# Layer B's memory queries and gates as four more paired products kept in DRAM, and the memory attention moved ahead of the sample attention

## The chip, the cores and the metric

The kernel runs on one core of a Trainium2 chip. The metric is the time of one execution on the device in microseconds. The time of the kernel before is 1783.64 us, the median of three runs (1783.11 to 1785.19).

## What is computed

One inference step of a trunk of two layers, A and then B, for a prompt of 512 tokens and a sample group of 8 x 8 = 64 tokens; the model width is 2048. Both groups share all weights, so that most products run over 576 columns. Layer A is a convolution module and is not touched. Of layer B this matters:

```python
def _b_layer(x, attend, mem_kv, w_in, w_out, ln_g, ln_b):
    h = jnp.einsum('btd,de->bte', x, w_in)
    q, gate, qm, gm = jnp.split(h, [MIX_WIDTH, MIX_WIDTH + B_OUT, MIX_WIDTH + B_OUT + MEM_WIDTH], axis=-1)
    q = q.reshape(b, t, N_GROUPS, B_HEADS_PER_GROUP, HEAD_DIM)
    o = attend([q[:, :, g] for g in range(N_GROUPS)])
    o = o.astype(x.dtype).reshape(b, t, B_OUT) * jax.nn.silu(gate)
    m = _mem_attn(qm, mem_kv) * jax.nn.silu(gm)
    y = jnp.einsum('bte,ed->btd', jnp.concatenate([o, m], axis=-1), w_out)
    return _layernorm(ALPHA * x + y, ln_g, ln_b)
```

`attend` is a dilated sliding-window attention with three groups of four heads of 128, merged by their softmax denominators. The sample group reads its keys and values from caches (`state_kv_g0` to `g2`). `_mem_attn` is a softmax attention of four heads over 256 memory entries (`qm` are its queries, `gm` its gate): for the prompt from `mem_prompt`, for the sample from `cache_mem_kv`. Inputs and outputs are float32.

## The kernel before

**Products.** Activations stand with the features on the partitions: 16 tiles of 128 features x 576 tokens. A weight slab is [128, 2048] for 128 output features. Each float32 factor is split into a high part in fp32r (copied on ScalarE, `wh`) and the rest (subtracted on VectorE, `wl`), and a product is three matmuls: high x high, high x low, low x high. A `Unit` is one slab, that is 4 steps (quarters of the slab); a step is 4 weight tiles x 3 products x 2 column halves of 288 = 24 matmuls. A `Pair` forms two slabs at once by a scheme of the Strassen kind: the two slabs, the two halves of the features and the two halves of the tokens are 2 x 2 blocks, and 7 block products stand for 8. It has 14 sets (7 products, two parts each) of 12 matmuls of 288 columns. For them VectorE forms eight sums of weight quarters (`sum`), in places given by `SUMS`, and the sums of the activations stand ready in `combos`. The evictions are in `after`: ScalarE copies an accumulator to a snapshot tile (`st`, in one of the two weight buffers with the tag `raw`), and VectorE adds a second accumulator in the function `evs`.

**The order.** `steps` is one list, and `run_steps` emits it: the matmuls of a step, the hooks at that place, the splits of the next steps, the eviction of the step before, and then `stage_lanes`, in which each of five lanes (queues of Python generators) does its next piece up to a `yield`. A turn of the lanes behind a step is called a stage here. Each engine runs its instructions in that order.

**Layer B.** First come the queries and keys of the attention, 24 slabs: 4 as units, then 20 as 10 pairs (`n_pairs` to `n_rest`). They are evicted to SBUF, written to the DRAM tile `kept_qk` on POOL's queue, and read back by `prompt_attn` on SP's queue. Then, from `n_rest` to `n_b`, come 12 units for the values, 8 for the memory's queries and gates (`B_QM`, `B_GM`: two queries, two gates, twice) and 4 for the attention's gate, 96 steps in all. Behind them stand the output units.

In that stage the lanes do the attention. Lane 0: `prompt_attn(h)`, from the moment the values of head h are there; it takes ten stages a head. Lane 1: `samples()`, for the two pairs of heads first the keys of three groups (`sample_keys`, 12 chunks), then one chunk more and 13 chunks of values (`sample_rest`), and at the end the memory attention of the sample (`queries_mem` with `mem_sample`, 4 chunks a pair). Lane 2: transposes of the values, and the gating. Lanes 3 and 4: the prompt's memory attention (`fetch_mem`, `mem_prompt`), started by the eviction of the gate (`start_mem`), and the split of its output (`mem_out`).

**The chunks.** The sample's caches are read in chunks of [128, 2048] float32, 1 MB. `chunk_load` issues their loads on POOL's queue, in the order of `chunk_list`, into two buffers:

```python
    def chunk_load():
        while cstate["load"] < min(cstate["use"] + 2, cstate["limit"]):
            ...
            t_ = kvp[0].tile([128, 2048], F32, tag="kv", bufs=2, name=f"kv{i}")
            nc.gpsimd.dma_start(t_, src)
```

A load waits on POOL until the matmuls that read the buffer's last chunk have ended. `sample_keys` and `sample_rest` take one chunk and then yield, so that a step's 24 matmuls (and what lane 0 has) stand between two chunks. The memory's keys and values for the prompt were formed in layer A's time and lie in the DRAM tile `spill`. SP's queue carries the weights, the saved queries and keys, the bias tables (`tp_`, `tl_`) and `spill`, in the order of the program.

Of the kernel before, what the change touches and what calls it, by code (L numbers as in the profile page):

```python
# [81 lines left out]
def trunk(ctx, tc, xt, memt, wm, wa, wao, wb, wbo, cst, scv, kc, rest, mc, relb, oneh,  # L82
# [420 lines left out]
    chunk_list += [mc[0, p_, c] for p_ in range(2) for c in range(4)]  # L503
    for p_ in range(2):
        chunk_list += [kc[p_, c] for c in list(range(1, 13)) + [0] + list(range(13, 26))]
    chunk_list += [mc[1, p_, c] for p_ in range(2) for c in range(4)]
# [613 lines left out]
    def fetch_mem(pr):  # L1120
# [3 lines left out]
        for a in range(2):  # L1124
            h = 2 * pr + a
            kmem1[h] = t_[:, a, :]
            nc.sync.dma_start(kmem1[h], spill[h])
            vs.append(u([128, NMEM], name="mkv"))
            nc.sync.dma_start(vs[a], spill[4 + h])
        yield  # L1130
# [8 lines left out]
        for a in range(2 * pr):  # L1139
            for h in (2 * a, 2 * a + 1):  # L1140
                lanes[4].append(mem_out(h))
# [274 lines left out]
    def sample_keys(pr):  # L1416
# [10 lines left out]
        for i in (1, 2, 3):  # L1427
            g = 1 if i == 1 else 2
            lg = at()
            for b in range(4):  # L1430
# [4 lines left out]
                if b < 3:  # L1435
                    yield
# [4 lines left out]
    def sample_rest(pr):  # L1441
# [40 lines left out]
        for i in range(13):  # L1482
# [9 lines left out]
            yield 0.25  # L1492
# [53 lines left out]
    def ev_qmb(h):  # L1546
        def f(ps):
            t_ = qmb[h] = u([128, T], name="qmb")
            nc.scalar.activation(two(t_), cols(ps), AF.Copy, scale=SCALE)
        return f  # L1550

    def start_mem(h):
        def f(ps):
            ev_gate(gmb, h)(ps)
            if h % 2:
                mem_ok[h // 2] = True
                lanes[3].append(fetch_mem(h // 2))
        return f
# [13 lines left out]
    for i in range(N_PLAIN, len(qks), 2):  # L1572
        two_ = qks[i:i + 2]
        add_pair(Pair([wb[row_qk(*it)] for it in two_], moving, [ev_qk(*it) for it in two_],
                      1.0 if two_[0][0] else SCALE))
    n_rest = len(steps)

    def samples():
        for _ in range(2):
            yield 0.0  # L1580
        for pr in range(2):
            yield from sample_keys(pr)
            yield from sample_rest(pr)
        for pr in range(2):
            yield from queries_mem(pr)
# [14 lines left out]
    for pr in range(2):  # L1600
        for h in (2 * pr, 2 * pr + 1):
            add_unit(unit_b(B_QM + h, ev_qmb(h)))
        for h in (2 * pr, 2 * pr + 1):
            add_unit(unit_b(B_GM + h, start_mem(h)))
# [234 lines left out]
    for k in range(4, KT):  # L1839
        hooks.setdefault((k - 4) // 4 * 2 + 1, []).append(lambda k=k: x_ready(k, None))  # L1840
    for k in range(8):
# [67 lines left out]
    lanes[1].append(samples())  # L1909
    run_steps(n_b)  # L1910
# [132 lines left out]
```

## Time and profile before

| | |
|---|---|
| median of 3 runs | 1783.64 us (1783.11 to 1785.19) |
| the profiled execution, its own time | 1783.62 us |
| its span, first to last instruction | 1781.8 us |
| granted TensorE clock, mean | 0.997 |
| TensorE busy | 1764.1 us, 99% of the span |
| VectorE, ScalarE, POOL busy | 1128.1, 726.5, 150.1 us (63%, 41%, 8%) |
| DMA | 368.08 MB, mean 207 GB/s |

The profile is of one execution; its own time and its span differ by 1.8 us that lie around the instructions. PE is TensorE, PEld its weight loads, DVE VectorE, ACT ScalarE, POOL GpSimd, SP SyncE; a q behind the name is the queue's own instructions. L1433 is line 1433 of the kernel. Matmuls are pipelined and their ends are modelled, so the distance from one to the next in the chain of waits says more than the duration of one. A releaser in brackets is what ended the wait ahead of an instruction. The DMA share is the mean busy share of the core's 16 DMA engines.

### The profile page before, as it was taken

The numbers are of one execution on the slowest core, as the hardware profiler recorded it, in microseconds if no ns is written. First come the engines' busy times: TensorE is split into PE (matmuls) and PEld (weight loads), VectorE is DVE, ScalarE is ACT, GpSimd is POOL, SyncE is SP. The second block draws the span as 40 slices with busy tenths as digits, with TensorE's granted clock in tenths as the row PEclk, the third lists the DMA queues.
The fourth block names the chain that finished last, engine by engine and source line by source line (L and its number), as shares of the span: only waits on it lengthen the run. The fifth ranks groups of instructions, "written<-read, shape, count | busy, mean of one in ns | idle before, by whom it ended". The sixth has DMA issues, their size and how long they took to land.

```text
span 1781.8 us, 34785 instructions
## 1 busy us (share of the span) xinstructions
PE 1764.1 (99%) x14134; PEld 1690.0 (95%) x14134; DVE 1128.1 (63%) x1977; ACT 726.5 (41%) x1581; POOL 150.1 (8%) x271
## 2 busy tenths in 40 slices
PE   8999999999999999999999999999999999999998
PEld 8999999999999999999999999997888789999997
DVE  6977998288999784546689777761322332324666
ACT  6444444355454452223476444442322232334334
POOL 0222221000000000000010000011111110001000
PEclk9999999999999999999999999999999999999999
DMA  8575678665556456466574555469787777435312
GB/s 303 184 260 180 215 230 281 202 213 207 183 202 208 155 184 224 173 209 216 197 231 153 201 201 201 143 216 322 253 320 261 263 294 256 151 131 178 108 52 102
DMA packets 98896, 368.08 MB, mean 207 GB/s; under 512 B 17888, under 2 KB 27136, under 8 KB 87345
## 3 DMA queue, kind: packets, MB, share of 16 engines
q1 hardware_dynamic: 70752, 256.95, 43.0%
q0 software_dynamic: 24528, 105.76, 16.7%
q10 hardware_dynamic: 3456, 3.15, 0.5%
q8 instruction: 111, 1.82, 0.4%
q14 instruction: 49, 0.39, 0.1%
HBM read 335.02 MB, written 125.43 MB: 258 GB/s over the span
## 4 chain that ended last, share of the span: by engine, by line
PE 96%; DMA 2%; DVE 1%; issue 0%; ACT 0%; ACTq 0%; SPq 0%; POOL 0%; DVEq 0%; POOLq 0%
PE pp L423 73%; PE pp L234 8%; PE pp L237 4%; DMA kv<-kc 2%; PE at L1488 1%; PE at L1433 1%; PE at L618 1%; PE at L596 1%; PE at L1370 1%; PE at L1368 1%; PE at L663 0%; PE at L643 0%; PE at L611 0%; PE at L1391 0%; PE at L1381 0%
## 5 line engine op out<-in xcount | busy, mean ns | idle before, releaser
L357 ACT CAST wh<-raw 128x512 fp32r<-128x512 f32 x410 | 247.3, 617 | 359.4 <-DMA raw<-wa 141.6
L368 DVE TENSOR_TENSOR wl<-raw,wh 128x512 fp32r<-128x512 f32 x410 | 278.3, 686 | 154.9 <-ACT wh L357 76.1
L423 PE MATMUL pp<-xh,wh 128*128 128x288 f32 (+2 forms) x1408 | 307.3, 300 | 6.3 <-ACT xh L524 6.3
L423 PE MATMUL pp<-xh,wl 128*128 128x288 f32 (+2 forms) x1408 | 303.3, 297 | 0.0
L423 PE MATMUL pp<-xl,wh 128*128 128x288 f32 (+2 forms) x1408 | 303.2, 297 | 0.0
L822 DVE SCALAR_TENSOR_TENSOR conv<-ep,consts,conv 128x512 f32<-128x512 f32 x360 | 269.6, 749 | 6.9
L423 PEld LDWEIGHTS pp<-xh,wh 128*128 128x128 f32 x1408 | 234.0, 190 | 9.4 <-ACT xh L524 6.3
L423 PEld LDWEIGHTS pp<-xh,wl 128*128 128x128 f32 x1408 | 234.2, 190 | 0.0
L423 PEld LDWEIGHTS pp<-xl,wh 128*128 128x128 f32 x1408 | 233.9, 190 | 0.3 <-DVE xl L525 0.3
L423 PE MATMUL pp<-cath,wh 128*128 128x288 f32 (+2 forms) x640 | 140.5, 297 | 0.0
L423 PE MATMUL pp<-cath,wl 128*128 128x288 f32 (+2 forms) x640 | 139.7, 296 | 0.0
L423 PE MATMUL pp<-catl,wh 128*128 128x288 f32 (+2 forms) x640 | 139.5, 296 | 0.0
L423 PE MATMUL pp<-yab,wh 128*128 128x288 f32 x512 | 134.3, 305 | 0.0
L357 ACT CAST wh<-rawq 128x512 fp32r<-128x512 f32 x140 | 86.5, 620 | 84.3 <-PE pp L234 57.4
L368 DVE TENSOR_TENSOR wl<-rawq,wh 128x512 fp32r<-128x512 f32 x140 | 95.7, 686 | 26.0 <-PE pp L237 22.3
L423 PE MATMUL pp<-yb,wh 128*128 128x288 f32 x384 | 107.4, 294 | 0.0
L423 PEld LDWEIGHTS pp<-cath,wh 128*128 128x128 f32 x640 | 104.1, 189 | 0.8 <-issue 0.3
L423 PEld LDWEIGHTS pp<-cath,wl 128*128 128x128 f32 x640 | 104.0, 189 | 0.0
L423 PEld LDWEIGHTS pp<-catl,wh 128*128 128x128 f32 x640 | 104.0, 189 | 0.0
L423 PEld LDWEIGHTS pp<-yab,wh 128*128 128x128 f32 x512 | 90.7, 188 | 13.9 <-issue 10.3
L795 ACT ACTIVATE prod<-es,consts 128x64 f32<-128x64 f32 x360 | 103.0, 343 | 1.3 <-ACT mkv L563 1.3
L423 PE MATMUL pp<-yh,wh 128*128 128x288 f32 x448 | 99.8, 304 | 0.2 <-ACT yh L1245 0.2
(326 smaller groups left out, 3238.8 us busy)
## 6 DMA issues: line engine op xcount, KB each, us to landing
o_kc<-kc SPq DMA_DIRECT2D x104, 512.0 KB, 5.9
kv<-kc POOLq DMA_DIRECT2D x52, 1024.0 KB, 6.7
raw<-wa SPq DMA_DIRECT2D x86, 512.0 KB, 4.7
o_rest<-rest SPq DMA_DIRECT2D x64, 512.0 KB, 6.4
raw<-wb SPq DMA_DIRECT2D x55, 512.0 KB, 5.4
rawq<-wb SPq DMA_DIRECT2D x80, 256.0 KB, 5.3
kv<-mc POOLq DMA_DIRECT2D x16, 1024.0 KB, 5.2
raw<-wao SPq DMA_DIRECT2D x32, 512.0 KB, 4.9
```

Source lines behind the costliest of these rows:

```text
L234: nc.tensor.matmul(o, hi[:, kk * 128:(kk + 1) * 128], self.move(x, g * 4 + kk, part), start=(fresh and kk == 0 and part == 0), stop=False, ...
L237: nc.tensor.matmul(o, lo[:, kk * 128:(kk + 1) * 128], self.move(x, g * 4 + kk, 0), start=False, stop=(g == 1 and kk == 3), skip_group_chec ...
L357: nc.scalar.copy(hi, r)
L368: nc.vector.tensor_tensor(lo, r, cast(hi), op=OP.subtract)
L423: nc.tensor.matmul(un.ps[:, c, :n], w[wi], xs[k][:, c0:c0 + n], start=(q == kk == a == 0), stop=(last and kk == 3 and a == 2 and not un.tail))
L596: nc.tensor.matmul(lg[:, a * 256:(a + 1) * 256], q[:, t0:t0 + 128], kt, start=True, stop=True)
L618: nc.tensor.matmul(o[:, 0:256], vt[:, kk, :], PT[:, kk * 256:(kk + 1) * 256], start=(kk == 0), stop=(kk == 1))
L795: nc.scalar.activation(dst, es[:, :, k:k + 8], AF.Copy, scale=w)
L822: nc.vector.scalar_tensor_tensor(cv[:, 0:TP], ep[:, k:k + TP], w, cv[:, 0:TP], op0=OP.mult, op1=OP.add)
L1368: nc.tensor.matmul(o, lhs, kk, start=True, stop=True, tile_position=(0, 32 * a))
L1370: nc.tensor.matmul(lg[:, 128 + 128 * g:256 + 128 * g], q_[g, h][:, r * 128:(r + 1) * 128], k_[g, h][:, r * 128:(r + 1) * 128], start=True, ...
L1433: nc.tensor.matmul(lg[32 * rg:32 * rg + 32, :], qe[g][:, rg * 128 + b * 32:rg * 128 + b * 32 + 32], ck[:, rg, :], start=(b == 0), stop=(b ...
```

## The change

Four pairs are appended to the ten: the memory's queries of heads 0 and 1, of heads 2 and 3, then the gates of the same. Their eviction `ev_m` adds the two parts on VectorE, applies SiLU in place for a gate, and writes each head's [128, 576] tile to the new DRAM tile `kept_m` on POOL's queue. The eight units that formed them go, with `ev_qmb` and `start_mem`, so that the stage from `n_rest` to `n_b` has 64 steps. `fetch_mem` now also loads the queries and gates of its two heads on SP's queue; the first call is put on lane 3 right behind the last pair, and the first call puts the second on the lane. In `samples` the memory attention (`queries_mem`, 8 chunks, still one to a stage) comes first, and in `chunk_list` its chunks do too. `sample_keys` yields behind every second chunk, and so does `sample_rest`. The splits of the memory attention's output (`mem_out`) are started by a hook 16 steps ahead of `n_b`. The two chunk buffers stay as they are.

```diff
@@ -501,9 +501,9 @@
         return t_
 
     chunk_list += [mc[0, p_, c] for p_ in range(2) for c in range(4)]
+    chunk_list += [mc[1, p_, c] for p_ in range(2) for c in range(4)]
     for p_ in range(2):
         chunk_list += [kc[p_, c] for c in list(range(1, 13)) + [0] + list(range(13, 26))]
-    chunk_list += [mc[1, p_, c] for p_ in range(2) for c in range(4)]
 
 
     copies = [(o_rest[i], rest[i]) for i in range(32)] + [(o_kc[p_, c], kc[p_, c]) for p_ in range(2) for c in range(26)]
@@ -1127,6 +1127,10 @@
             nc.sync.dma_start(kmem1[h], spill[h])
             vs.append(u([128, NMEM], name="mkv"))
             nc.sync.dma_start(vs[a], spill[4 + h])
+            for kind, d in enumerate((qmb, gmb)):
+                d[h] = u([128, T], name="qgm")
+                nc.sync.dma_start(d[h], kept_m[kind, h])
+        mem_ok[pr] = True
         yield
         v = u([128, 2, 2, HD], name="mv")
         for a in range(2):
@@ -1136,9 +1140,8 @@
         for a in range(2):
             h = 2 * pr + a
             lanes[3 + a].append(mem_prompt(qmb[h], kmem1[h], vmem1[h], h, sink_mem))
-        for a in range(2 * pr):
-            for h in (2 * a, 2 * a + 1):
-                lanes[4].append(mem_out(h))
+        if pr == 0:
+            lanes[3].append(fetch_mem(1))
 
     def queries_mem(pr):
 
@@ -1432,7 +1435,7 @@
                 for rg in range(4):
                     nc.tensor.matmul(lg[32 * rg:32 * rg + 32, :], qe[g][:, rg * 128 + b * 32:rg * 128 + b * 32 + 32],
                                      ck[:, rg, :], start=(b == 0), stop=(b == 3), tile_position=(0, 32 * rg))
-                if b < 3:
+                if b == 1:
                     yield
             nc.vector.tensor_tensor_reduce(L[i], lg, L[i], scale=1.0, scalar=LOWEST, op0=OP.add, op1=OP.max,
                                            accum_out=mx[:, i:i + 1])
@@ -1489,7 +1492,9 @@
                                      pe[i % 2][:, rg * 128 + b * 32:rg * 128 + b * 32 + 32], cv[:, rg * 4 + b, :],
                                      start=(i == 0 and b == 0), stop=False, tile_position=(0, 32 * rg),
                                      skip_group_check=True)
-            yield 0.25
+            if i % 2:
+                yield 0.25
+        yield 0.25
         while not vdone[pr]:
             yield 0.0
 
@@ -1543,18 +1548,22 @@
 
     qmb, gmb, mob, gtb = [None] * 4, [None] * 4, [None] * 4, [None] * 4
 
-    def ev_qmb(h):
-        def f(ps):
-            t_ = qmb[h] = u([128, T], name="qmb")
-            nc.scalar.activation(two(t_), cols(ps), AF.Copy, scale=SCALE)
-        return f
-
-    def start_mem(h):
-        def f(ps):
-            ev_gate(gmb, h)(ps)
-            if h % 2:
-                mem_ok[h // 2] = True
-                lanes[3].append(fetch_mem(h // 2))
+    kept_m = tc.dram_tile([2, 4, 128, T], F32, name="kept_m")
+
+    def ev_m(kind, h):
+
+        got = {}
+
+        def f(c, src, add):
+            if not got:
+                got["t"] = u([128, T], name="m")
+            d = got["t"][:, c * 288:(c + 1) * 288]
+            nc.vector.scalar_tensor_tensor(d, src, 1.0 if kind else SCALE, add, op0=OP.mult, op1=OP.add)
+            if kind:
+                nc.scalar.activation(d, d, AF.Silu)
+            got[c] = True
+            if 0 in got and 1 in got:
+                nc.gpsimd.dma_start(kept_m[kind, h], got["t"])
         return f
 
     def unit_b(row, ev):
@@ -1573,16 +1582,20 @@
         two_ = qks[i:i + 2]
         add_pair(Pair([wb[row_qk(*it)] for it in two_], moving, [ev_qk(*it) for it in two_],
                       1.0 if two_[0][0] else SCALE))
+    for kind in range(2):
+        for h in (0, 2):
+            add_pair(Pair([wb[(B_GM if kind else B_QM) + h + a] for a in range(2)], moving,
+                          [ev_m(kind, h + a) for a in range(2)], 1.0 if kind else SCALE))
     n_rest = len(steps)
 
     def samples():
-        for _ in range(2):
+        for _ in range(3):
             yield 0.0
+        for pr in range(2):
+            yield from queries_mem(pr)
         for pr in range(2):
             yield from sample_keys(pr)
             yield from sample_rest(pr)
-        for pr in range(2):
-            yield from queries_mem(pr)
 
     first = True
     for h in range(4):
@@ -1597,11 +1610,6 @@
             un.spare = u if first else None
             first = False
             add_unit(un)
-    for pr in range(2):
-        for h in (2 * pr, 2 * pr + 1):
-            add_unit(unit_b(B_QM + h, ev_qmb(h)))
-        for h in (2 * pr, 2 * pr + 1):
-            add_unit(unit_b(B_GM + h, start_mem(h)))
     for h in range(4):
         add_unit(unit_b(B_GT + h, chain(ev_gate(gtb, h), (2, gate_o(h)))))
     n_b = len(steps)
@@ -1838,6 +1846,8 @@
         hooks.setdefault(n_mk - 10 + j, []).append(lambda j=j: sp_mem(j))
     for k in range(4, KT):
         hooks.setdefault((k - 4) // 4 * 2 + 1, []).append(lambda k=k: x_ready(k, None))
+    for h in range(4):
+        hooks.setdefault(n_b - 16, []).append(lambda h=h: lanes[4].append(mem_out(h)))
     for k in range(8):
         hooks.setdefault(n_rest - 5, []).append(lambda k=k: restore(k, 0))
         hooks.setdefault(n_rest - 1 + k // 4, []).append(lambda k=k: restore(k, 1))
@@ -1907,6 +1917,7 @@
     chunk_load()
     run_steps(n_rest)
     lanes[1].append(samples())
+    lanes[3].append(fetch_mem(0))
     run_steps(n_b)
     drain(1)
     scopes["kv"].close()
```

## Rows read from the trace of the kernel before

**Rows 1.** The page: engines over the span, and the chain that ended last.

```profile
PE 1764.1 (99%) x14134; PEld 1690.0 (95%) x14134; DVE 1128.1 (63%) x1977; ACT 726.5 (41%) x1581; POOL 150.1 (8%) x271
...
PE 96%; DMA 2%; DVE 1%; issue 0%; ACT 0%; ACTq 0%; SPq 0%; POOL 0%; DVEq 0%; POOLq 0%
```

**Rows 2.** Stretches: length, then PE, PEld, DVE, ACT, POOL busy, PEclk, DMA share, GB/s.

```profile
1038.00:1194.00 156.00, 156.00 (x1180) 156.00 (x1179) 116.10 (x207) 68.47 (x125) 13.90 (x26) 1.00 0.51 174
1206.00:1262.00 56.00, 53.40 (x399) 40.72 (x398) 11.04 (x26) 13.18 (x25) 8.09 (x15) 1.00 0.90 326
1300.00:1320.00 20.00, 19.40 (x244) 17.25 (x236) 3.63 (x9) 4.53 (x8) 2.70 (x5) 1.00 0.99 372
1366.00:1431.00 65.00, 65.00 (x522) 50.83 (x524) 17.01 (x45) 15.97 (x37) 8.12 (x15) 1.00 0.81 290
```

**Rows 3.** TensorE's groups, 1190 to 1650 us: busy, mean ns, idle before, releaser.

```profile
L1488 PE MATMUL at<-kv,pe 128*32 128x128 f32 x832 | 28.1, 276 | 0.6 <-DMA kv<-kc 0.6
L1433 PE MATMUL at<-kv,qe 128*32 128x512 f32 x192 | 25.6, 604 | 2.6 <-DMA kv<-kc 2.6
```

**Rows 4.** The chain of waits in the pairs: start us, us, what.

```profile
1150.80 1.07 PE pp L234 x8
...
1173.06 1.07 PE pp L234 x8
```

**Rows 5.** The same chain: the first value steps, and eight plain steps.

```profile
1193.74 12.74 PE pp L423 x96
...
1557.89 25.46 PE pp L423 x192
```

**Rows 6.** DMA issues, 1038 to 1262 us: KB each, us to landing.

```profile
kept_qk<-qk POOLq DMA_DIRECT2D x14, 256.0 KB, 2.8
...
kv<-kc POOLq DMA_DIRECT2D x12, 1024.0 KB, 7.3
...
L<-tl__92 SPq DMA_DIRECT2D x3, 256.0 KB, 5.6
```

**Rows 7.** The chain of waits where chunks are read, 1366 to 1503 us.

```profile
1366.93 1.00 PE at L1433 x8
1367.93 3.37 PE pp L423 x24
...
1425.71 0.99 PE at L1433 x8
...
1438.80 1.01 PE at L1488 x32
...
1502.96 1.01 PE at L1488 x32
```

**Rows 8.** The timeline: one chunk's read, and the load into its buffer.

```profile
1206.41 1.06 PE L1433 MATMUL at<-kv,qe 128*32 128x512 f32 x8
...
1207.81 0.55 POOL L492 DMA_DIRECT2D kv<-kc  x1 [9.30 <-PE at L1433]
```

**Rows 9.** Chunk loads, L492, from 1195 to 1510 and 1560 to 1600 us.

```profile
DMA to landing us min/median/max: 5.0/6.8/9.2
...
DMA to landing us min/median/max: 5.1/5.2/5.2
```

**Rows 10.** DMA queues (packets, MB, share) and chunk issues, 1366 to 1510 us.

```profile
q0 software_dynamic: 4071, 28.16, 54.4%
q1 hardware_dynamic: 4872, 12.05, 23.8%
...
kv<-kc POOLq DMA_DIRECT2D x24, 1024.0 KB, 6.5
...
kv<-mc POOLq DMA_DIRECT2D x2, 1024.0 KB, 8.7
```

**Rows 11.** The timeline of SP's queue behind the last pair.

```profile
1196.68 0.33 SPq L337 DMA_DIRECT2D raw<-wb  x1
...
1202.51 1.85 SPq L1421 DMA_DIRECT2D L<-tl__92  x4
```

## Prediction

> **What bounds the kernel now.** The page first: TensorE is busy for 99% of the span, and the chain of work that ended last is TensorE for 96% and DMA for 2% [rows 1]. So a matmul left out counts in full, as long as nothing else makes TensorE wait. Then the stretches one by one [rows 2]: from 1038 to 1194 us (layer B's pairs) TensorE never idles, VectorE has 116.10 us of 156, ScalarE 68.47, and the DMA share is 0.51. In the stage behind it, where the caches are read, VectorE and ScalarE are nearly free but the DMA queues are not: share 0.90 and 326 GB/s in the first run of key chunks, 0.99 and 372 GB/s in the densest 20 us, 0.81 later. Even so TensorE waits little there: 2.6 us before key chunks, 0.6 us before value chunks [rows 3]. That is one chunk of 1 MB to a stage, and two buffers.
>
> **The products.** One of a pair's 14 sets (12 matmuls) follows another after 1.59 us; 14 of them go from 1150.80 to 1173.06, 22.26 us [rows 4]. Eight plain steps, the work of two plain units, take 25.46 us [rows 5]. Four pairs in place of eight units: 4 x (22.26 - 25.46) = **-12.8 us**, if the pairs stay dense. VectorE's 116.10 of 156 us are 16.6 us of a pair's 22.26 [rows 2]; the new pairs' splits and weight sums are the same, their evictions no larger than the keys' now. The gates add two short SiLU passes a head, and at worst a table load, on ScalarE, which is busy for 44% there. The eight writes to DRAM go out on POOL's queue like those of the saved queries and keys, which land in 2.8 us [rows 6] and keep nobody waiting. I cost all this at nothing: TensorE's own matmuls hide it. Without that cover a pair would lose what VectorE needs beyond 22.26 us, and it has 5.6 us to spare.
>
> **What the missing steps take with them.** They are also time in which cache chunks arrive. The stage has 96 steps now and 64 afterwards. By the order of the program (each lane moves on once behind each step) the attention's keys and values are now read in 52 stages of one chunk; afterwards in 24 stages of two, in four runs, and four of one.
>
> TensorE's need: key chunks start at 1366.93 and, eleven stages on, at 1425.71, 5.34 us each with prompt attention and value transposes; value chunks go from 1438.80 to 1502.96 in twelve, 5.35 us [rows 7]. A second chunk adds 1.00 us [rows 7], so a stage of two wants **6.4 us**; bare of prompt attention 3.37 + 1.00 + 1.00 = 5.4 us.
>
> The buffer's need: the two chunks of a stage are read back to back, and the load into the second's buffer can't go out before that read has ended. A read that starts at 1206.41 takes 1.06 us, and its successor's load is issued at 1207.81, 0.34 us behind its end [rows 8]. From issue to landing a load takes 5.0 us at the least, 6.8 in the median and 9.2 at the most in this stage, and 5.1 to 5.2 where the queues are quiet [rows 9]. So the second buffer comes round in 0.34 + L + 1.06 us:
> - L = 5.1: 6.5 us, about TensorE's 6.4. Only stages bare of attention lose, 1.1 us each; three to eight of them, say 6 us in all.
> - L = 6.8: 8.2 us, 1.8 us lost in a stage.
> - L = 7.3, the median of the crowded first run [rows 6]: 8.7 us, 2.3 us lost.
>
> The first stage of each run finds both chunks loaded, which leaves 20 stages: 6, 36 or 46 us. Today the same round may take two stages, 10.7 us, which is why it is nearly hidden.
>
> A check by bytes: from 1366 to 1510 us the two queues moved 28.16 + 12.05 MB, of which 26 chunks (24 of keys and values, two of the memory [rows 10]) are 27.3; so 12.9 MB of weights, saved queries and keys, bias and outputs went beside them in 27 stages, 0.48 MB each. A stage of two needs 2.1 + 0.48 = 2.58 MB: at the best rate seen, 372 GB/s, 6.9 us, a loss of 0.5 x 20 = 11 us; in 8.2 us it is 315 GB/s, between the 290 and 326 GB/s of the two runs of key chunks [rows 2]. So L = 6.8 is what the queues deliver. Now most loads fly alone for a part of their way, then two are always under way at once, which argues against less; the wait itself spreads them, which argues against much more. **+36 us**, with 6 and 46 as bounds.
>
> By a page of the Trainium skill (DMA: Bandwidth & Descriptors, section "Anatomy of one DMA — SWDGE (gpsimd) path") a load costs a fixed 2.0 us and its bytes at 436 GB/s, an estimate of 4.4 us for a chunk; the shortest landing here is 5.0 us [rows 9]. By that figure the buffer would come round in 5.8 us, and the sum would be that of the first rival.
>
> **Smaller terms.** The waits of today go with their stages: -(2.6 + 0.6) = **-3.2 us** [rows 3]. A step behind a chunk takes 3.37 us, another 3.18 (25.46 / 8) [rows 7, 5]; 24 fewer such places give 0 to 24 x 0.19 = 4.6, I take the middle, **-2.3 us**. With two value chunks in a stage, the second's weights are transposed and copied while the first is multiplied; that copy is short, VectorE is free, and the second chunk is late anyway: nothing.
>
> The opening: the loads of the memory's keys, values, queries and gates for heads 0 and 1 are issued in the very first stage, and TensorE transposes those values one stage later. SP is not ahead there: its weight loads wait for buffers that the pairs' snapshots hold, and the second of them goes out at 1196.68; behind that one come eight new loads. The four that stand at 1202.51 now take 0.46 us each to issue [rows 11] and land after 5.6 us [rows 6]. So the sixth of the eight (head 1's values) goes out at 1196.7 + 0.3 + 5 x 0.46 = 1199.3 and lands at 1204.9; TensorE is there after two steps, 1193.74 + 6.4 = 1200.1 [rows 5]. **+4.8 us**; nothing, if SP has run ahead; 9.5, if the first read has to wait until the last gates are written. The next weights stand behind those eight loads, 3.7 us later than now, inside the same wait. For heads 2 and 3 SP has run far ahead by then: nothing. The chunk list's new order and the earlier hook for the memory's split are the same loads and operations on engines that wait: nothing.
>
> **Sum.** The profiled execution took 1783.62 us, the median of the runs is 1783.64, so nothing is corrected. 1783.6 - 12.8 - 3.2 - 2.3 + 36 + 4.8 = 1806.1: **1806 us**, 1.3% slower.
>
> **Rivals.**
> 1. *The loads stay hidden and the saving remains.* One mechanism, the time from issue to landing: at 5.1 us the buffer comes round as fast as TensorE wants it. 1783.6 - 18.3 + 6 + 0 to 4.8 = 1771 to 1776, **1774 us**, faster. For it: 5.1 us is what a load takes in quiet queues, and in the second half the median was 6.5, not 7.3 [rows 10, 6]. Against it: its partner is always under way too, and the best 20 us would already ask for 6.9 us a stage. It decides from L of about 5.7 us down, where the loss, (5.7 + 1.4 - 6.4) x 20 = 14 us, and the opening together equal the gain.
> 2. *Bandwidth alone counts.* The queues are kept full and a stage takes 6.9 us: 1783.6 - 18.3 + 11 + 4.8 = **1781 us**, no change that can be told. For it: a share of 0.99 was held for 20 us [rows 2]. Against it: with two buffers the second load is not under way while its predecessor is being read.
> 3. *Crowded throughout.* L goes to 7.3 and the opening costs 9.5: 1783.6 - 18.3 + 46 + 9.5 = **1821 us**. For it: in the first run of keys that was the median, and now twice the chunks come in a stage. Against it: the memory attention stands first, and takes the crowded opening stages with one chunk each.
> 4. *The change doesn't do what it says*: VectorE or the writes to DRAM hold the pairs up. The dense stretch speaks against it, and it would only add to the slower side; no chance of its own.
>
> **Chances.** Forecast 0.55, rival 1 0.16, rival 2 0.09, rival 3 0.20. A measurement tells 0.2% (3.6 us) from no change. Faster: rival 1 and a third of rival 2, 0.19. Same: most of the rest of rival 2, 0.05. Slower: 0.76. The range leaves out half of rival 1 below and a part of rival 3 above, about 2 in 10: 1773 to 1824 us. The forecast's own is 1794 to 1817.
>
> **What the profile would show.** Pairs: four more at 22.3 us each with no idle TensorE, so that the value units start 89 us later, near 1283 us. Opening: some us of idle TensorE before the transposes of the memory's values. Cache reading: TensorE idle for 1 to 3 us in most two-chunk stages, at the second chunk, ended by the DMA into the chunk tile, 30 to 45 us in all; a median landing of about 6.8 us; a DMA share above 0.85 in the runs. The prediction is wrong if landings stay near 5 us with two in flight, if TensorE's idle time there is under 18 us, or if the pairs' stretch shows idle TensorE.

## The result, and the profile after

The changed kernel takes 1833.24 us, median of four runs (1827.37 to 1838.5), beside 1784.2 us before: 1.026 times as long, 95% interval 1.0229 to 1.0291. The forecast was 1806 us, range 1773 to 1824: the direction is right, the loss more than twice as large as foretold, and the time outside the range. The profiled execution took 1830.15 us, 46.5 us more than that of before.

In what follows, before and after name the two kernels. TensorE by stretches (length, busy, granted clock, DMA share, GB/s): first, of before, the 500 us from the end of its pairs on; then, of after, the pairs (with the busy times of the four other engines), ten microseconds of the opening, the 410 us behind the pairs, and the same 500 us as of before:

```profile
1190.00:1690.00 500.00, 496.25 (x4595) 1.00 0.66 234
```

```profile
1038.00:1283.00 245.00, 245.00 (x1851) 245.00 (x1850) 180.99 (x318) 110.16 (x201) 19.23 (x36) 1.00 0.47 158
...
1290.00:1300.00 10.00, 5.49 (x28) 0.66 0.54 202
...
1280.00:1690.00 410.00, 362.98 (x3474) 0.95 0.71 256
1190.00:1690.00 500.00, 452.98 (x4153) 0.96 0.65 233
```

The pairs, now fourteen, run without a gap until 1283 us, 89 us later than the 1194 us of [rows 2], as foretold. Behind them TensorE is idle for 500 - 452.98 = 47.0 us, where it was idle for 3.75. And the granted clock, 1.00 there before, is 0.95 on the mean of 410 us: since its levels are 1 and 0.5 of 2.4 GHz, 410 x 0.05 / 0.5 = about 41 us at 1.2 GHz (the single stretches add up to 44).

What ended the idle time, TensorE's groups of after from 1280 to 1700 us (busy, mean ns of one, idle before and releasers):

```profile
L1491 PE MATMUL at<-kv,pe 128*32 128x128 f32 x832 | 31.1, 295 | 17.8 <-DMA kv<-kc 14.8 <-DVE wl L368 1.6 <-DVE pe L1482 1.4
L1436 PE MATMUL at<-kv,qe 128*32 128x512 f32 x192 | 28.3, 679 | 20.7 <-DMA kv<-kc 20.7
L618 PE MATMUL at<-mpt,mv 128*128 128x256 f32 x32 | 8.6, 392 | 1.8 <-DVE ob L626 1.4 <-DVE p L1388 0.5
L548 PE MATMUL at<-consts,mkv 128*128 128x128 f32 x8 | 2.0, 367 | 5.8 <-DMA mkv<-spill 5.8
```

These are the groups of [rows 3]: the wait for chunks went from 0.6 + 2.6 to 14.8 + 20.7 = 35.5 us, the opening's transposes wait 5.8, and some 5.5 us are waits that VectorE ends. The reads of the keys also became slower by themselves: 604 ns a matmul in [rows 3], 679 here. The timeline of after shows why, here TensorE alone around two stages (start, duration, what, idle before and its releaser):

```profile
1407.21 1.07 PE L1436 MATMUL at<-kv,qe 128*32 128x512 f32 x8 [1.05 <-DMA kv<-kc]
1410.34 1.34 PE L1436 MATMUL at<-kv,qe 128*32 128x512 f32 x8 [2.06 <-DMA kv<-kc]
...
1413.00 0.68 PE L423 MATMUL pp<-yl,wh 128*128 128x288 f32 x2
1413.48 0.68 PE L423 MATMUL pp<-yh,wl 128*128 128x288 f32 x2
...
1414.97 0.42 PE L423 MATMUL pp<-yh,wh 128*128 128x288 f32 x2
1415.23 0.42 PE L423 MATMUL pp<-yl,wh 128*128 128x288 f32 x2
...
1421.16 1.91 PE L1436 MATMUL at<-kv,qe 128*32 128x512 f32 x8 [2.33 <-DMA kv<-kc]
```

Ahead of 1411 us TensorE waited 1.05 and 2.06 us for the two chunks of one stage. Then a pair of plain matmuls follows its predecessor after 0.48 us; from 1414.4 us on it is 0.26 us again. The chunk read at 1421.16, behind another wait, takes 1.91 us for its 8 matmuls, not 1.07. The granted clock says the same (of the plain matmuls alone the busy time, that of their weight loads, then clock, share, GB/s):

```profile
1400.00:1405.00 5.00, 3.44 (x24) 3.20 (x24) 1.00 0.80 269
1405.00:1411.00 6.00, 0.00 (x0) 0.00 (x0) 1.00 1.00 397
1411.00:1414.40 3.40, 2.03 (x8) 2.10 (x9) 0.50 1.08 419
1414.40:1421.00 6.60, 2.31 (x18) 2.07 (x16) 1.00 1.03 389
```

There are ten such stretches between 1280 and 1690 us, one behind the opening's wait and nine behind waits for chunks. At 0.48 for 0.26 us, some 45% of a stretch is lost, 44 x 0.45 = about 20 us; by the starts of all matmuls in them it is 20 as well. Not each wait is followed by one: behind waits for chunks of 2.07 us (ahead of 1511 us) and 2.36 us (ahead of 1518 us) the clock stayed at 1.00.

So the 46.5 us are: pairs -12.8, the idle time of before -3.7, idle time of after +47.0, matmuls at 1.2 GHz about +20, and about -4 that is left over; the missing places of a step behind a chunk would lie in it.

The loop that sets the pace here, in after's chain of waits (start, us, what):

```profile
1410.34 1.36 PE at L1436 x8
1411.70 0.28 issue
1411.98 9.13 DMA kv<-kc
...
1421.16 1.94 PE at L1436 x8
1423.09 0.28 issue
1423.38 5.09 DMA kv<-kc
...
1429.91 7.75 DMA kv<-kc
```

It is read, issue, load and read again of one and the same buffer, and nothing of TensorE's other work stands in it. A round takes 11.4 us here (1411.98 to 1423.38) and 6.5 to 1429.91. In the long round the bytes have their part: the DMA share was 1.00 to 1.08 all the while (table above), and the load took 9.13 us; the next one took 5.09. The landings from 1395 to 1660 us:

```profile
DMA to landing us min/median/max: 5.0/6.5/9.4
```

### The profile page after: what moved, and what is told of

Read it like the earlier page. It is cut to its first block, busy times and chain, and to the rows that moved or that the text cites. A ratio compares the mean times of both kernels' runs of the same rounds, so it can differ in the third digit from the quotient of the medians.

```text
span 1828.4 us, 34789 instructions
## 1 busy us (share of the span) xinstructions
PE 1768.0 (97%) x14038; PEld 1691.2 (92%) x14038; DVE 1172.0 (64%) x2053; ACT 740.7 (41%) x1614; POOL 154.4 (8%) x279
## 4 chain that ended last, share of the span: by engine, by line
PE 86%; DMA 8%; issue 4%; DVE 1%; ACT 1%; POOL 0%; SPq 0%; ACTq 0%; POOLq 0%; DVEq 0%
PE pp L423 60%; PE pp L234 11%; DMA kv<-kc 6%; PE pp L237 6%; PE at L1491 1%; DMA raw<-wb 1%; PE at L1436 1%; PE at L618 1%; PE at L596 1%; PE at L643 0%; DVE wl L368 0%; PE at L663 0%; PE pp L1040 0%; PE at L964 0%; DMA mkv<-spill 0%
## 5 line engine op out<-in xcount | busy, mean ns | idle before, releaser
L357 ACT CAST wh<-raw 128x512 fp32r<-128x512 f32 x378 | 227.8, 617 | 309.4 <-DMA raw<-wa 139.2
L368 DVE TENSOR_TENSOR wl<-raw,wh 128x512 fp32r<-128x512 f32 x378 | 256.3, 685 | 127.1 <-ACT wh L357 67.7
L357 ACT CAST wh<-rawq 128x512 fp32r<-128x512 f32 x196 | 120.6, 619 | 112.3 <-PE pp L234 74.2
L368 DVE TENSOR_TENSOR wl<-rawq,wh 128x512 fp32r<-128x512 f32 x196 | 134.2, 687 | 38.1 <-PE pp L237 31.8
L423 PE MATMUL pp<-cath,wl 128*128 128x288 f32 (+2 forms) x640 | 139.7, 296 | 0.0
L234 PE MATMUL pp<-comb,wh 128*128 128x288 f32 x896 | 136.9, 294 | 0.0
L234 PEld LDWEIGHTS pp<-comb,wh 128*128 128x128 f32 x896 | 125.0, 188 | 0.0
L423 PE MATMUL pp<-yab,wh 128*128 128x288 f32 x384 | 100.5, 312 | 0.0
L423 PEld LDWEIGHTS pp<-yab,wh 128*128 128x128 f32 x384 | 69.2, 194 | 9.5 <-issue 8.5
```

Of the source, the lines that this page charges most:

```text
L234: nc.tensor.matmul(o, hi[:, kk * 128:(kk + 1) * 128], self.move(x, g * 4 + kk, part), start=(fresh and kk == 0 and part == 0), stop=False, ...
L357: nc.scalar.copy(hi, r)
L368: nc.vector.tensor_tensor(lo, r, cast(hi), op=OP.subtract)
L423: nc.tensor.matmul(un.ps[:, c, :n], w[wi], xs[k][:, c0:c0 + n], start=(q == kk == a == 0), stop=(last and kk == 3 and a == 2 and not un.tail))
```

## The experiments

The theory: each two-chunk stage waits for its buffers' round, and behind the waits the clock falls to 1.2 GHz, which costs as a second term. The rivals are named in the expectations: A, what else the change does makes the loss (the missing steps, the order); B, the queues can't deliver the bytes, whatever the buffers; C, the clock costs nothing of its own; D (from the two pairs on), any shortening of this stage is given back. Beside each run stand times of before on the same chip (medians of 1782.7 to 1787.4 us); the ratios are to those.

### The two-chunk yields alone, on the kernel before

```diff
-                if b < 3:
+                if b == 1:
                     yield
...
-            yield 0.25
+            if i % 2:
+                yield 0.25
+        yield 0.25
```

> The kernel before with one part of the change alone: the sample's keys and values are read two chunks to a stage. No pairs, the 96 steps stay, the memory attention stays last. Theory (two buffers that come round once in a stage, and a TensorE clock that falls behind the waits): the same 20 stages wait, 30 to 50 us of idle TensorE at the second chunk, granted clock below 1.00 in the stretches behind them, 1784 + 35 to 65 = 1820 to 1850 us. Rival A (the loss comes from the missing 32 steps, in which the caches' bytes arrive): all 96 steps are there, so little is lost, 1784 to 1795 us.

1836.91 us (1834.36 to 1838.93), ratio 1.0292 (1.027 to 1.0314). With all 96 steps and no new pair the loss is there in full. Its groups, and its stretches (all engines, then clock, share, GB/s):

```profile
L1488 PE MATMUL at<-kv,pe 128*32 128x128 f32 x832 | 31.5, 298 | 19.4 <-DMA kv<-kc 12.5 <-DVE new L1327 2.4 <-DVE pe L1479 2.2
L1433 PE MATMUL at<-kv,qe 128*32 128x512 f32 x192 | 28.0, 669 | 20.8 <-DMA kv<-kc 20.7
...
1190.00:1500.00 310.00, 269.82 (x2664) 226.95 (x2663) 74.77 (x208) 69.99 (x159) 37.45 (x70) 0.93 0.75 274
1500.00:1660.00 160.00, 160.00 (x1336) 151.43 (x1334) 48.81 (x114) 53.20 (x111) 6.16 (x12) 1.00 0.38 129
```

40 us of idle time and some 41 us at 1.2 GHz (ten stretches), all before 1500 us; then, to 1660 us, TensorE is never idle again, since the chunks are used up early. The loss doesn't need rival A: pairing the chunks makes the loss, with every step in place. That the missing steps would make it too, without the pairing, is what the run with one chunk to a stage shows (below).

### Useless matmuls in the wait

Ahead of the second chunk of 20 stages stand 14 matmuls that nobody reads; everything else is as in after.

```diff
+    def fill():
+        d_ = at()
+        for _ in range(14):
+            nc.tensor.matmul(d_[:, 0:288], onesr, yh[15][:, 0:288], start=True, stop=True)
...
+                if b % 2 and (i, b) != (1, 1):
+                    fill()
...
+            if i % 2 and i > 1:
+                fill()
```

> The changed kernel with work added: ahead of the second chunk of a stage (not in the first stage of a run) 14 matmuls of 288 columns whose result nobody reads, 1.8 us. Theory (the clock falls behind idle stretches and costs about 20 us of slower matmuls): the added matmuls stand mostly in time that was a wait, the granted clock stays at 1.00 in more of the stage, and the time falls although TensorE has 36 us more to do: 1815 to 1830 us, with low-clock time of under 20 us where it was 44. Rival C (the matmuls are slower because the transfers crowd them, not because of the clock): low-clock time as before, and the time rises by what of the 36 us doesn't fit into waits, 1835 to 1850 us.

1831.23 us (1827.83 to 1833.47), ratio 1.0255 (1.0229 to 1.028): as long as after, with 280 matmuls more, and 1 us above the band that the theory expected. Its groups, and its stage:

```profile
L1422 PE MATMUL at<-yh,ones 128*128 128x288 f32 x280 | 43.4, 307 | 4.1 <-DVE pe L1489 4.1
L1500 PE MATMUL at<-kv,pe 128*32 128x128 f32 x832 | 28.1, 275 | 4.5 <-DMA kv<-kc 4.4
L1443 PE MATMUL at<-kv,qe 128*32 128x512 f32 x192 | 25.8, 616 | 5.3 <-DMA kv<-kc 5.2
...
1280.00:1690.00 410.00, 387.00 (x3738) 0.99 0.71 257
```

The idle time is 23 us where it was 47, the clock 0.99, and the chunks are read at 616 and 275 ns, nearly as in [rows 3]. At 0.13 us from start to start (plain matmuls at full clock, above) the 280 are at least 37 us of work; 24 fit into idle time, and the other 13 are paid by matmuls that are back at full speed. Rival C falls: had the clock cost nothing, the kernel would be 13 us longer.

### Half chunks, split by column group

Four buffers of 0.5 MB, each freed when its half is read; for that the read goes group by group.

```diff
-            t_ = kvp[0].tile([128, 2048], F32, tag="kv", bufs=2, name=f"kv{i}")
+                t_ = kvp[0].tile([128, 1024], F32, tag="kv", bufs=4, name=f"kv{i}_{hf}")
...
-            for b in range(4):
-                for rg in range(4):
+            for rg in range(4):
+                for b in range(4):
```

> The changed kernel with each 1 MB chunk loaded as two tiles of 0.5 MB into four buffers of half the size (the same bytes, the same SBUF), and read half by half, so that a buffer is free again after half the read. Theory (the buffer's round trip is the limit): a half needs about 3.8 us from issue to landing when alone, its buffer comes round in 0.34 + 3.8 to 5 + 0.53 = 4.7 to 5.9 us, below the 6.4 us of a stage: idle TensorE at the caches falls from about 40 to under 15 us, the clock stays at 1.00 in most stretches, 1780 to 1800 us. Rival B (the queues' bandwidth is the limit): the bytes are the same and twice as many loads have to be started, so the waits stay, 1825 to 1840 us.

1862.51 us (1857.92 to 1871.3), ratio 1.0442 (1.0407 to 1.0477): a miss, some 60 us above the theory's band and above that of rival B too.

```profile
L1493 PE MATMUL at<-kv,pe 128*32 128x128 f32 x832 | 66.5, 276 | 1.4 <-DMA kv<-kc 1.1
L1438 PE MATMUL at<-kv,qe 128*32 128x512 f32 x192 | 41.1, 646 | 15.7 <-DMA kv<-kc 15.7
```

The chunk waits halved, 35.5 to 16.8 us, but the 832 value matmuls are busy for 66.5 us and not 31.1: one takes 276 ns as in [rows 3], so what they lost is running side by side. The cut changed the order of the reads along with the buffers, and tells nothing of the buffers alone.

### Half chunks, split by columns

Four buffers of 0.5 MB again, but each half holds a part of all four groups, so that the order of the groups stays; the loads have pieces of 1 KB.

```diff
+                t_ = kvp[0].tile([128, 4, 256], F32, tag="kv", bufs=4, name=f"kv{i}_{hf}")
+                nc.gpsimd.dma_start(t_, src.rearrange("p (g n) -> p g n", g=4)[:, :, hf * 256:(hf + 1) * 256])
```

> The changed kernel with each chunk in two tiles of 0.5 MB and four buffers of half the size, as in the run with half chunks, but cut so that each half holds a part of all four column groups: the four matmuls that ran side by side in the array still do, and a read takes 1.0 us again. Price: each partition's row comes in four pieces of 1 KB in place of one of 4 KB. Theory (the round trip of a buffer makes the waits): a half's buffer comes round in 0.34 + 4 to 5.5 + 0.5 = 4.8 to 6.3 us, under the 6.4 us of a stage; idle TensorE at the chunks falls from 35 to 5 to 18 us, low-clock time from 44 to under 25 us, 1790 to 1812 us. Rival B (bandwidth of the queues): 2.58 MB still have to come in a stage, in smaller pieces, so the waits are 35 us or more and the time 1830 us or more.

1840.76 us (1838.88 to 1857.62), ratio 1.0332 (1.0281 to 1.0383), and chunk waits of 38.8 us:

```profile
L1496 PE MATMUL at<-kv,pe 128*32 128x128 f32 x832 | 34.1, 299 | 19.2 <-DMA kv<-kc 17.2 <-DVE pe L1487 2.0
L1439 PE MATMUL at<-kv,qe 128*32 128x256 f32 x384 | 29.1, 407 | 21.6 <-DMA kv<-kc 21.6
```

The time and the waits are those of rival B. The theory counted on halves that land in 4 to 5.5 us; from 1400 to 1640 us they land after 6.4 us in the median, hardly sooner than the whole chunks of after (6.7). The pieces have a part in that: the queue's share was 61.8% for 50.68 MB, where after has 59.1% for 52.31, 8% more for a byte. So a finer grain of the same 2 MB doesn't help; how much of that is the bytes and how much the 1 KB pieces, this run leaves open.

### The opening two stages later

```diff
-        yield
+        for _ in range(1 if pr else 3):
+            yield
```

> The changed kernel with the first transposes of the memory's values two stages later (the loads are issued where they were). Theory (the opening waits 6.5 us for loads that are issued one stage before they are read, and the clock falls behind that wait): both go, 6.5 us and some 3 us of slow matmuls, 1833 - 10 = 1823 us; no idle TensorE before the transposes. Rival (the loads are late for another reason, as the wait for the last gates to be written): the wait is still there, 1833 us.

1833.05 us (1829.76 to 1846.09), ratio 1.0285 (1.0243 to 1.0327): no gain, and the 1823 us of the theory not met, though the wait is gone from its place.

```profile
1290.00:1300.00 10.00, 9.19 (x76) 1.00 0.79 276
...
L643 PE MATMUL at<-kv,qe 128*32 128x256 f32 x64 | 5.0, 386 | 3.5 <-DVE qe L1152 3.5
L1437 PE MATMUL at<-kv,qe 128*32 128x512 f32 x192 | 29.9, 719 | 20.2 <-DMA kv<-kc 20.2
```

The stretch that had 5.49 us of TensorE has 9.19, at full clock. But 3.5 us of waiting for the copy of the memory's queries come in place, and the chunk waits grew to 20.2 + 20.3 = 40.5: in this run the stage takes back what is won ahead of it.

### One chunk to a stage

After with the old yields, so that some 17 value chunks are left when the 64 steps are over, and are read with no product beside them.

> The changed kernel with the yields of the kernel before: one chunk to a stage. The lane then needs about 83 stages and 64 are there; what is left over, about 17 chunks of values, is read at the end of the stage with no steps in between. Theory: in the steps no waits but the opening's 6 us; at the end each chunk costs about the 2.5 to 4 us that its transfer takes, 45 to 65 us, nearly all of it idle, and the clock falls there: 1771 + 6 + 45 to 65 + 10 = 1832 to 1852 us. Rival B (the bytes set the time): whatever the order, the same loss as in the changed kernel, 1825 to 1838 us.

1832.45 us (1820.3 to 1841.04), ratio 1.0253 (1.0209 to 1.0297). Its stretch without steps (62 us), and the one with steps:

```profile
1627.00:1689.00 62.00, 35.29 (x463) 26.05 (x464) 6.53 (x19) 1.38 (x2) 7.55 (x14) 0.50 0.68 249
1400.00:1600.00 200.00, 198.20 (x1900) 167.26 (x1899) 61.74 (x163) 62.15 (x132) 22.70 (x42) 1.00 0.77 279
```

With one chunk to a stage two buffers do, 1.8 us idle in 200; the price stands at the end in one piece. So the 60 chunks cost about the same whether the 32 missing stages are missing under them or behind them. Both expectations had room for this time, so it doesn't decide between them.

### Two pairs in place of four

Heads 0 and 1 by pairs, heads 2 and 3 by the old units: 80 steps, one chunk to a stage, the memory attention behind each pair's sample attention.

```diff
-        for h in (0, 2):
+        for h in (0,):
             add_pair(Pair([wb[(B_GM if kind else B_QM) + h + a] for a in range(2)], moving,
...
+    for h in (2, 3):
+        add_unit(unit_b(B_QM + h, ev_qmb(h)))
+    for h in (2, 3):
+        add_unit(unit_b(B_GM + h, start_mem(h)))
```

> Half of the change, built so that no run of chunks needs two in a stage: only heads 0 and 1 get their memory queries and gates from pairs and DRAM, heads 2 and 3 stay units, so that 80 steps remain; the keys and values are read one chunk to a stage again, but for the first stage of each run, whose two chunks have landed before; the memory attention of each pair of heads comes behind its sample attention; the first transposes come three stages later than in the changed kernel. Theory: two pairs save 6.4 us, the chunks wait about as little as in the kernel before (3 to 6 us), the clock stays at 1.00: 1783 - 6.4 = 1774 to 1780 us. Rival D (any shortening of this stage is given back, because the caches' bytes set its length): 1782 to 1800 us.

1790.22 us (1786.26 to 1803.97), ratio 1.0028 (1.0001 to 1.0056): level at best, 10 us above the theory and in the range of rival D. Half the saving, 6.4 us, is eaten by 10.7 us of chunk waits, 6 of them in the crowded opening, and 2.9 ahead of the first memory read, most of which the profile gives no releaser for:

```profile
L1493 PE MATMUL at<-kv,pe 128*32 128x128 f32 x832 | 28.1, 275 | 4.2 <-DMA kv<-kc 2.8 <-DVE pe L1484 1.4
L1438 PE MATMUL at<-kv,qe 128*32 128x512 f32 x192 | 26.0, 622 | 7.9 <-DMA kv<-kc 7.9
...
L643 PE MATMUL at<-kv,qe 128*32 128x256 f32 x64 | 4.9, 418 | 2.9 <-issue 2.7 <-DVE qe L1153 0.2
```

### A third buffer

Four tiles of 128 x 512 are free in this stage: together one chunk. This separates the buffers' round from the bytes with rows of 2 KB and more.

```diff
+            if third and (i - third[0]) % 3 == 0:
+                for j, t_ in enumerate(third[1]):
+                    nc.gpsimd.dma_start(t_, src[:, j * 512:(j + 1) * 512])
+                ctiles[i] = third[1]
...
+    def third_open():
+        third.extend([cstate["load"], [u([128, 512], name="third") for _ in range(4)]])
+        nbuf[0] = 3
```

> The kernel after with a third chunk buffer from the tenth step behind the last pair on (four free tiles of 128 x 512, so that every third chunk comes in four loads of 256 KB with 2 KB rows); reads, yields and everything else unchanged. My theory (the round trip of a buffer through load and read makes the waits, and the clock falls behind the waits): with three buffers a load has three chunks' time, 1.5 stages or 9.6 us, against the 8.2 us it needs, so the 35.5 us of chunk waits fall to between 0 and 11 us (the bytes want 6.9 us a stage at the best rate seen, TensorE 6.4), the ten stretches at 1.2 GHz with them to one to three; the opening's 5.8 us stay. Time 1833 - 25 to 35 - 15 to 20 = 1778 to 1793 us. Rival B (the DMA queues cannot deliver two chunks a stage, however many buffers): waits of 25 us or more remain, and the time stays above 1815 us.

1801.6 us (1794.93 to 1811.96), ratio 1.0062 (1.0038 to 1.0085): 32 us better than after, 9 us above the expected band. Its groups and its stage:

```profile
L1501 PE MATMUL at<-kv,pe 128*32 128x128 f32 x544 | 18.4, 275 | 6.9 <-DVE pe L1492 4.4 <-DMA kv<-kc 2.5
L1446 PE MATMUL at<-kv,qe 128*32 128x512 f32 x128 | 16.6, 602 | 6.9 <-DMA kv<-kc 6.9
L1446 PE MATMUL at<-third,qe 128*32 128x512 f32 x64 | 13.8, 601 | 3.4 <-DMA third<-kc 3.4
L1501 PE MATMUL at<-third,pe 128*32 128x128 f32 x288 | 9.9, 276 | 1.4 <-DVE pe L1492 1.4
...
1190.00:1690.00 500.00, 472.81 (x4351) 0.98 0.67 239
```

The chunk waits went from 35.5 to 12.8 us, and the ten stretches at 1.2 GHz to four: most of the loss was the round of two buffers, and the clock behind it. It isn't that loads got faster: from 1400 to 1640 us a whole chunk lands after 8.3 us in the median, in after 6.7; with three buffers there is time for that. Rival B explains the rest at most: the 12.8 us are about what the bytes were expected to want, up to 11 us, and from 5 us ahead of each of these waits to its end the DMA share is 0.81 to 1.03. That every third chunk comes in four loads was not tried apart. What I had not expected are four waits of 1.4 us for VectorE's copy of the second chunk's weights, which now shows, since that chunk is there in time.

The same buffer on the kernel before:

> The kernel before with the third chunk buffer alone. It tells how much of what the two other kernels of this call win is the buffer's own. Its chunk waits are 3.2 us; theory: they vanish, 1780 to 1784 us, no change that can be told. If loads of 256 KB or three in flight cost something by themselves, it is slower by 4 us or more.

1785.63 us (1779.8 to 1794.9), ratio 0.9992 (0.9968 to 1.0016): no change, as expected; where chunks hardly wait it wins nothing.

### Four pairs with the other waits mended as well

The third buffer, the opening two stages later with a stage between the query copy and its use, and both weights of a stage made at the end of the stage before.

```diff
-            if i < 12:
-                weights(i + 1)
...
             if i % 2:
+                for j in range(i + 1, min(i + 3, 13)):
+                    weights(j)
                 yield 0.25
```

> The four pairs with three chunk buffers, and the two other waits mended that the version with three buffers alone still shows: the transposes of the memory's values two stages later and one stage between the copy of the memory queries and their use (5.9 us at the opening), and both softmax weights of a stage transposed and copied at the end of the stage before, not the second one between the two reads (5.7 us in four waits that VectorE's copy ends). If these waits are costs of their own, as each on its page stands, it takes 1801.6 - 5.9 - 5.7 - about 5 (half clock behind the opening) = 1785 us, 1780 to 1790, level with the kernel before: the saving of 18 us is then eaten by some 13 us of chunk waits that the bytes leave. If the bytes are the bound, the chunk waits take up the time freed, and it stays at 1795 to 1802 us.

1799.18 us (1793.03 to 1804.47), ratio 1.0076 (1.0046 to 1.0106): the second case of the expectation.

```profile
1190.00:1690.00 500.00, 478.02 (x4441) 1.00 0.67 242
```

The mended waits (5.9 and 5.7 us) are gone, yet the idle time fell only from 27.2 to 22.0: chunk waits are 15.7, up from 12.8, and others of VectorE 5. The clock in the stage is 1.00. How much that wins isn't settled. In the two profiled executions the first output matmul starts at 1651.8 us and, with the third buffer alone, at 1665.0; but that one was the longest of its eight (1811.96 us), and the medians of all runs hardly differ (1799.18 and 1801.6 us, ratios 1.0076 and 1.0062). So the chunks took back some 3 us in the profile; whether they take back all that is mended ahead of them, as the medians suggest, stays open. What stays is that 60 chunks in 64 steps come some 16 us late even with three buffers.

### Two pairs with the third buffer

The version with two pairs, the third buffer, the first read-back 16 steps later, and a stage between the query copy and its use.

```diff
-    lanes[3].append(fetch_mem(0))
+    hooks.setdefault(n_rest + 16, []).append(lambda: lanes[3].append(fetch_mem(0)))
...
+        yield 0.0
         yield from mem_sample(pr, sink_mem)
```

> The version with two pairs (memory queries and gates of heads 0 and 1 alone, one chunk to a stage) with the third chunk buffer, its first read-back of memory values 16 steps later, out of the crowded opening, and one stage between the copy of the memory queries and their use. In that version 10.7 us of chunk waits and 3.0 us behind the query copy stood against a saving of 6.4 us. My theory: both go, 1790 - 10 to 14 - 2 to 5 (clock) = 1772 to 1779 us, faster than both kernels. Rival B (bytes, not buffers): some 8 us of waits remain, 1785 to 1790. Rival D (what is saved in the stage returns as a lower clock in the last stage): the waits go and the time still stays above 1782 us.

1779.44 us (1772.27 to 1787.81, twelve runs; before beside it 1787.43), ratio 0.9957 (0.9935 to 0.998): 0.4% faster than before, clear of the interval, and faster than after. Its one group with idle time, and its stage:

```profile
L1449 PE MATMUL at<-kv,qe 128*32 128x512 f32 x152 | 20.9, 627 | 4.2 <-DMA kv<-kc 4.2
...
1190.00:1690.00 500.00, 495.84 (x4573) 0.99 0.68 241
```

The stage waits hardly more than before's (4.2 us for 3.75), so the two pairs' saving of 6.4 us is kept, and rival D falls in both its forms. Which of the three additions did how much of it was not tried apart.

## Why the prediction was right and wrong

**The products**: right. Fourteen dense pairs, no idle TensorE from 1038 to 1283 us, and neither VectorE nor the writes held them up: -12.8 us.

**The chunk waits**: +36 us foretold, 35.5 measured; landings of 6.8 foretold, 6.5 in the median. The DMA share, foretold above 0.85, is 0.85 in the first run of keys (1405 to 1448 us) and 0.77 to 0.81 in the later runs. The mechanism holds: the chain is load, read and issue of one buffer, and a third buffer takes 23 of the 35.5 us away. The single stages are less even than 20 equal waits of 1.8 us: a round took from 6.5 to 11.4 us, and the first chunk of a stage waits too (1407.21). That the sum fits so well owes something to these evening out. The estimate of 4.4 us a load from the Trainium skill (DMA: Bandwidth & Descriptors, section "Anatomy of one DMA — SWDGE (gpsimd) path") was again not met: the shortest landing is 5.0 us, and the measurement decides.

**The opening**: +4.8 foretold, 5.8 measured. SP was not ahead, and the values land 6.54 us after their issue, not 5.6:

```profile
1287.25 1.28 SPq L1127
1288.62 6.54 DMA mkv<-spill
```

**The step that failed is the sum itself**: "1783.6 - 12.8 - 3.2 - 2.3 + 36 + 4.8". It charges each idle microsecond as one microsecond, and takes the matmuls between the waits at the speed of before, whose clock was 1.00 throughout [rows 2]. There is no term for what idle time does to the work behind it: about 44 us at 1.2 GHz, a loss of some 20 us, of the 24 us by which the profiled execution exceeds the forecast. All bounds of the range came from the landing time and the opening, so that 1824 us was its end. With the term the forecast would have been about 1826 us. The useless matmuls show that it is a cost of its own, and that it hangs on the waits. The Trainium skill (TensorE: Matmul & The Clock Gate, section "HAM oscillation — how this bites in real kernels") has the rule that I left out, from one kernel there: matmuls in bursts with DMA waits between them run each burst at half clock anew. The trace agrees in part: ten stretches at 0.50, behind waits like the 1.05 and 2.06 us ahead of 1411 us, but none behind the 2.07 and 2.36 us ahead of 1511 and 1518 us.

**Smaller steps**: the copy of the second chunk's weights was costed at "nothing", since "the second chunk is late anyway". That held (1.4 us in after); it is 5.7 us as soon as the chunk is in time. Other waits that VectorE ends, 4 us, I had not seen. The missing places of a step behind a chunk, -2.3 foretold, were not measured by themselves; about -4 is left over.

**The rivals**: the loads did not stay hidden (1). Bandwidth alone (2) would have cost 11 us: that is near what three buffers leave (12.8 and 15.7), so it fits as a floor under the round. Rival 3's time, 1821 us, is the nearest of the list, but not by its mechanism: neither the landing was 7.3 us nor the opening 9.5.

The profile shows less of the trouble than the time does: TensorE is busy for 1768.0 us in after, more than the 1764.1 of [rows 1] in spite of fewer matmuls, since slow matmuls count as busy.

## What to carry to other kernels

A saving of steps is also a loss of time in which transfers hide: ask, before removing work, what arrives under it, and whether another buffer is free for it; here half the change, with four free tiles as a buffer and the opening's waits moved away, won 0.43%, the whole change lost 2.6%. Charge short, repeated waits of TensorE at their own length and also at what the clock does to the work behind them; here that added some 40% to the waits' own length (20 to 47 us). Where a wait stayed, work put into it cost nothing here (1831.23 us with it, 1833.24 without).

## What the runs showed of the hardware that was not expected

Behind waits of 1 to 4 us, one or two in a row, came stretches at 1.2 GHz, ten in after; with matmuls in those waits the mean clock is 0.99. The wait's length alone doesn't decide: behind 2.34 us, ahead of 1473 us, the clock fell, behind 2.36 us, ahead of 1518 us, it didn't. In the run with one chunk to a stage, TensorE stayed at 0.50 for the 62 us in which chunks were read with no product beside them.

Matmuls of 128 x 32 tiles in different column groups run side by side: 832 of 276 ns each are busy for 28 us when the groups alternate (two pairs with two buffers), for 66.5 us when four of one group stand together. That is a factor of 2.4.

The last stage, which is untouched by all this, ran at half clock for 25 to 30 us in some of the profiles and for 3 to 6 us in the others, and this alone moves a run by some 8 us: from the first output matmul to the last it takes 139.7 us in the profile of the four mended pairs, where the clock fell, and 131.6 us in that of before. The 30 us in which it fell (mean clock 0.57, so 1.2 GHz most of the time):

```profile
1770.00:1800.00 30.00, 21.92 (x57) 0.57 0.25 92
```

The runs of before beside that kernel lie from 1781.13 to 1792.55 us, which fits: the three longest have a mean clock of 0.990 to 0.992, the others 0.997 and more. What decides it stays open.
